# State updates behind the level of 32, level 64 in the first level tensor, gate products one projection later

## The chip, the cores and the metric

One core of a Trainium2 chip runs the whole program; the other seven are idle. The metric is the device time of one execution in microseconds (us). Five engines work side by side: TensorE (PE in the profile; its weight loads are PEld), VectorE (DVE), ScalarE (ACT), GpSimd (POOL) and SyncE (SP, which issues DMAs). Each runs its instructions in the order in which they were put into its queue, and waits where one needs a result of another engine that isn't there.

## The reference, cut to what matters

One layer of a decoder takes 512 prompt tokens and 8 sample tokens (520 columns). The part that the change touches is two recurrences that share one input projection. HGRN2 has 8 heads with 128 keys and values:

```
S_t = diag(f_t) S_{t-1} + k_t outer v_t        o_t = S_t^T q_t
```

For the prompt it is computed in chunks; the 8 samples update a state of 128 x 128 each once. RG-LRU has 8 blocks of 128 channels, each with a causal convolution of width 4 and gates from block-diagonal matrices:

```
xc = causal_conv(xb);  r = sigmoid(blockdiag(xc, wa) + ba);  ig = sigmoid(blockdiag(xc, wx) + bx)
a = exp(-8 r softplus(-lambda));  h_t = a_t h_(t-1) + sqrt(1 - a_t^2) (ig_t xc_t)
o_b = h * gelu(yb)
```

Everything behind it (the merge of both branches, the output projection, the MLP) is left as it is.

## The kernel before, in words

Activations lie with channels on the 128 partitions and the 520 tokens along the free axis. Every projection (`gemm`) yields 128 channels: eight blocks of 128 inputs, for each three products (the weights' high part with the activations' high and low part, and the weights' low part `wlo` with the high part) of two halves of 260 columns, so 48 matmuls of L110. The weights come by DMA to `wst`; ScalarE casts the high part `whi` (L78) and VectorE subtracts it for `wlo` (L81). There are two places, so a projection's weights are split while the one before runs, and its fifth product is the first that reads `wlo`.

The heads come one after the other. Head h projects f, q, the output gate and v. An even head is followed by the projections of two x blocks (`rg_x`): each is evacuated to `xb`, goes through the convolution `xc` on VectorE (L732, and three pairs L735 and L736), is split into `xcs` (ScalarE L158, then VectorE), and enters the block-diagonal products (`blockdiag`, L718): first with `wa`, then with `wx`, three products for each half, whose results ScalarE turns into gates (L132). An odd head has the scans (`rg_scans`) of both blocks between its gate and its v, and the projections of two y blocks (`rg_y`) behind it. The scans use ScalarE functions of several tables, and so there are three table loads in each odd head: for L753 and L754, for the square roots L760, and back for the sigmoids L132.

Within a head (`head_prompt`) the prompt's decays are taken apart by levels of 1, 2, 4, 8, 16, 32 and 64 tokens. Each level multiplies half of the last level tensor by the decays and copies the other half (VectorE L568 and L572) into a new tile `Y` of a ring of four. Small fp32 products of 32 x 32 and 32 x 64 blocks (L582) fill the attention matrix; those of levels 8 to 32 and the state products of the samples form one group. `level(64)` yields the keys that L643 transposes; ScalarE copies these to `kn` (L645), which L649 multiplies by the values. Each head's sample part, `head_sample`, scales a state by f on ScalarE (L527) and adds key times value on VectorE (L528); the values come as `vb`, a broadcast to all partitions through DRAM (v to `vs`, to `vd`, to `vb`).

The program is written in tile form, and a scheduler puts each engine's instructions in order by priority, a simulated timeline and the tiles' dependencies. `urgent` raises the priority, `behind` keeps an instruction behind another in the order without a semaphore, and the small products are chained that way, behind the level and the state update that they read.

Of the kernel before, what the change touches and what calls it, by code (L numbers as in the profile page):

```python
# [6 lines left out]
F32 = mybir.dt.float32  # L7
# [4 lines left out]
OP = mybir.AluOpType  # L12
# [6 lines left out]
T = L + NB  # L19
HALF = T // 2  # L20
KO = D // 128
H = 8
C = 128
# [20 lines left out]
RING = 4  # L44
# [7 lines left out]
class Kernel:  # L52
    def __init__(self, ctx, tc, ins, outs):
# [1 line left out]
        self.i, self.o = ins, outs  # L55
        self.group, self.sigmoids, self.mod_open = None, [], None
        self.ppt_free = True


    def weights(self, specs):  # L60
        self.wspecs = specs
# [51 lines left out]
                    self.behind(self.last_product, after)  # L113

    def gemm(self, keys, acts, extra=0):

        ps = self.pmm.tile([128, 2, 512], F32, name="mm")
        for q, key in enumerate(keys):
            hi, lo = self.take_w(key)
            for k in range(KO):  # L120
                n = q * KO + k
                self.products(ps, (hi[:, k], lo[:, k]), acts[n], n == 0, n == len(keys) * KO - 1, extra)
                if self.mod_open and k == MODK:
                    self.mod_close(self.last_product)
        return ps


    def behind(self, ins, first):
        self.tc.add_manual_dep(ins.ins, first.ins.name, NOSYNC, reason="tables")

    def sigmoid(self, out, x, **kw):
        ins = self.nc.scalar.activation(out, x, AF.Sigmoid, **kw)  # L132
        if self.group:
            self.behind(ins, self.group)
        self.sigmoids.append(ins)
        return ins
# [384 lines left out]
                            vd.rearrange("b v -> (b v)").partition_broadcast(128))  # L521
        return vb

    def head_sample(self, h, st, vb, fkq):
        nc = self.nc
        for b in range(NB):
            nc.scalar.activation(st[:, b], st[:, b], AF.Copy, scale=fkq[:, 0, b:b + 1])  # L527
            last = nc.vector.scalar_tensor_tensor(st[:, b], vb[:, b], fkq[:, 1, b:b + 1], st[:, b], OP.mult, OP.add)  # L528
        nc.sync.dma_start(self.o["hgrn_s"][0, :, h].rearrange("b k v -> k b v"), st)
        return last  # L530

    def head_sample_out(self, h, ev):
        nc = self.nc
# [6 lines left out]
    def head_prompt(self, h, f, X, q, v, og, st, vb, fkq):  # L540
        nc = self.nc
# [14 lines left out]
        def view(t, first_q, first_k, step, n, b):  # L556

            return bass.AP(tensor=t.tensor, offset=t.offset + first_q,
                           ap=[t.ap[0], [T + first_k - first_q, 2], [step, n], [1, b]])

        levels, decay = [X], [f[:, :L], 0]

        def level(b):

            X, (tb, to), n = levels[-1], decay, L // (2 * b)
            Y = self.hg.tile([128, 2, T], F32, name="Y", bufs=RING)
            fac = bass.AP(tensor=tb.tensor, offset=tb.offset, ap=[tb.ap[0], [1, 2], [2, n], [0, b]])
            made = nc.vector.tensor_tensor(view(Y, b, 0, 2 * b, n, b), view(X, b, 0, 2 * b, n, b), fac, OP.mult)  # L568
            if b == 1:
                nc.scalar.copy(view(Y, 0, 1, 2, n, 1), view(X, 0, 1, 2, n, 1))  # L570
            else:
                made = nc.vector.tensor_copy(view(Y, 0, b, 2 * b, n, b), view(X, 0, b, 2 * b, n, b))  # L572
            t2 = tb.rearrange("p (n two) -> p n two", two=2)
            tn = T_[:, to:to + n]
            nc.vector.tensor_tensor(tn, t2[:, :, 0], t2[:, :, 1], OP.mult)
            levels.append(Y)
            decay[:] = tn, to + n
            return made
# [8 lines left out]
        def blocks(after, p, c0, x):  # L587
# [4 lines left out]
            return p[:, c0:c0 + 128].rearrange("p (c t) -> p c t", c=NC)  # L592

        level(1)
        made = [level(2)]
        p = self.pps.tile([128, 512], F32, name="ps")
        for c in range(NC):
# [7 lines left out]
        for b in (1, 2, 4):  # L605
            nc.vector.copy_predicated(a32, self.masks[b], found[b])

        level(4)
        level(8)
        state = self.head_sample(h, st, vb, fkq)  # L610
        level(16)
        made = [level(32), state]
        p = self.pps.tile([128, 512], F32, name="ps")
        p2 = self.ppt.tile([128, 512], F32, name="pt")
        for c in range(NC):
# [4 lines left out]
        for b in range(NB):  # L620
            j, c = 32 * (b % 4), 256 + 128 * (b // 4)
# [10 lines left out]
        nc.scalar.copy(at[:64, :, 64:], p2[:64, :256].rearrange("p (c t) -> p c t", c=NC))  # L632
        ev = self.hg.tile([128, 256], F32, name="sev", bufs=1)
        nc.scalar.copy(ev, p2[:, 256:])
        level(64)
        X, tb = levels[-1], decay[0]
        Q, K = X[:, 0], X[:, 1]
        for j in range(0, 128, 32):
# [71 lines left out]
    def blockdiag(self, w, x, bias):  # L710
        nc = self.nc
        o = self.slot(self.hg, "gate")
        (wh, wl), (xh, xl) = w, x
        for s in range(2):
            c = slice(s * HALF, (s + 1) * HALF)
            ps = self.ppb.tile([128, 512], F32, name="pb")
            for n, (a, b) in enumerate(((wh, xh), (wh, xl), (wl, xh))):
                nc.tensor.matmul(ps[:, :HALF], a, b[:, c], start=n == 0, stop=n == 2)  # L718
            self.sigmoid(o[:, c], ps[:, :HALF], bias=bias)
        return o  # L720

    def rg_x(self, n):

        nc = self.nc
        w = self.blockdiag_w(n)
        ps = self.gemm([(self.i["w_in"][0], 0, 4 * D + n * 128)], self.h)[:, :, :HALF]
        xb = self.slot(self.hg, "xb")
        with self.urgent():
            nc.scalar.copy(self.two(xb), ps)
        xc = self.slot(self.hg, "xc")  # L730
        cw = self.cw
        nc.vector.tensor_scalar(xc, xb, cw[:, 3, n:n + 1], self.cb[:, n:n + 1], OP.mult, OP.add)  # L732
        for j in range(3):
            d = 3 - j
            nc.vector.scalar_tensor_tensor(xc[:, d:L], xb[:, :L - d], cw[:, j, n:n + 1], xc[:, d:L], OP.mult, OP.add)  # L735
            nc.vector.scalar_tensor_tensor(xc[:, L:], self.cbuf[:, :, j, n], cw[:, j, n:n + 1], xc[:, L:],  # L736
                                           OP.mult, OP.add)
        nc.vector.tensor_copy(self.xlast[:, n, 0:3], xb[:, L - 3:L])
        nc.vector.tensor_copy(self.xlast[:, n, 3:11], xb[:, L:])
        xs = self.split(xc, self.hg, "xcs")  # L740
        r = self.blockdiag(w[0], xs, self.ba[:, n:n + 1])
        g = self.blockdiag(w[1], xs, self.bx[:, n:n + 1])
        nc.vector.tensor_tensor(g, g, xc, OP.mult)
        self.rg[n] = r, g

    def rg_scans(self, ns):
# [816 lines left out]
```

## Time and profile before

| | us |
|---|---|
| median of three runs | 1032.24 |
| lowest and highest | 1031.08, 1033.33 |
| the profiled execution | 1032.62 |
| its span, from the first to the last instruction | 1030.6 |
| TensorE busy in the span | 985.0 (96%) |
| VectorE, ScalarE, GpSimd busy | 691.3, 524.2, 112.1 |

In a row of the timeline the first number is the start in us from the span's start, the second the time to the end of the last of the instructions that are grouped in the row; in brackets is the idle time of the engine ahead of it, and what ended it. A row of the waits has the total in us, how often, and the longest. The eight heads with their x and y blocks end at about 440 us.

### The profile page before, as it was taken

To read this page: it belongs to the slowest core of one execution; us is meant where nothing else is said; L and a number is where in the kernel's file an instruction comes from. 1 tells how busy PE (TensorE), PEld (TensorE's weight loads), DVE (VectorE), ACT (ScalarE), POOL (GpSimd) and SP (SyncE) were. 2 spreads that over 40 slices of the span, in tenths; PEclk is the share of its full clock that TensorE was granted. 3 is DMA by queue.
4 is the path that set the end of the run, shared out by engine and by line. 5 is a ranking of instruction groups with operands and counts; after the bars stand their busy time and mean duration, and the time that the engine had idled before them with its cause. 6 is when DMAs were issued, how large, how long until landed. Compare 5 with 4: busy or idle time off the path is not lost.

```text
span 1030.6 us, 23395 instructions
## 1 busy us (share of the span) xinstructions
PE 985.0 (96%) x9620; PEld 956.8 (93%) x9620; DVE 691.3 (67%) x1533; ACT 524.2 (51%) x998; POOL 112.1 (11%) x217
## 2 busy tenths in 40 slices
PE   3899999999899899999999999999999999999995
PEld 1799998999899899998998999999999999999994
DVE  6669697686968687474333347677776776777675
ACT  5545753574466257352222235466556655656653
POOL 3200000000000000020000000011421331232040
PEclk9999999999999999999999999999999999999998
DMA  9944344343434424495755677322672483273242
GB/s 301 283 138 113 119 127 134 90 134 123 113 112 127 117 83 125 122 330 160 230 170 164 216 206 187 88 83 62 134 188 68 94 188 109 53 175 82 63 82 84
DMA packets 214508, 143.65 MB, mean 139 GB/s; under 512 B 6142, under 2 KB 200854, under 8 KB 214394
## 3 DMA queue, kind: packets, MB, share of 16 engines
q1 hardware_dynamic: 204498, 130.24, 42.7%
q0 software_dynamic: 9904, 11.92, 6.1%
q8 instruction: 75, 1.23, 0.5%
q14 instruction: 31, 0.25, 0.1%
HBM read 123.61 MB, written 11.26 MB: 131 GB/s over the span
## 4 chain that ended last, share of the span: by engine, by line
PE 83%; DVE 5%; ACT 3%; DMA 3%; issue 1%; DVEq 0%; ACTq 0%
PE mm L110 60%; PE ps L1101 8%; PE pt L1101 4%; PE pb L1101 2%; PE ps L352 1%; DMA vb<-vd 1%; PE pb L718 1%; DVE wlo L81 1%; PE ps L582 1%; DVE st L528 1%; PE mm L1101 1%; DMA vd<-vs 1%; PE pt L660 1%; PE pt L649 1%; DVE xc L735 1%
## 5 line engine op out<-in xcount | busy, mean ns | idle before, releaser
L110 PE MATMUL mm<-h,whi 128*128 128x260 f32 (+1 forms) x3072 | 508.7, 285 | 1.8 <-ACT X L132 1.2
L110 PEld LDWEIGHTS mm<-h,whi 128*128 128x128 f32 x3072 | 427.2, 189 | 5.0 <-issue 2.5
L110 PE MATMUL mm<-h,wlo 128*128 128x260 f32 (+1 forms) x1536 | 317.3, 285 | 4.5 <-DVE wlo L81 4.5
L78 ACT CAST whi<-wst 128x1024 fp32r<-128x1024 f32 x166 | 173.6, 1049 | 217.3 <-PE mm L110 166.1
L81 DVE TENSOR_TENSOR wlo<-wst,whi 128x1024 fp32r<-128x1024 f32 x166 | 202.9, 1223 | 89.9 <-ACT whi L78 86.8
L110 PEld LDWEIGHTS mm<-h,wlo 128*128 128x128 f32 x1536 | 240.8, 189 | 6.8 <-DVE wlo L81 5.8
L110 PE MATMUL mm<-a,whi 128*128 128x260 f32 x512 | 83.7, 284 | 0.0
L110 PEld LDWEIGHTS mm<-a,whi 128*128 128x128 f32 x512 | 70.5, 189 | 0.9 <-issue 0.8
L110 PE MATMUL mm<-a,wlo 128*128 128x260 f32 x256 | 52.3, 285 | 0.0
L813 POOL DMA_DIRECT2D t<-oaT_d x8 | 4.3, 550 | 389.7 <-ACT whi L78 382.8
L1197 DVE TENSOR_TENSOR f<-f 128x260 f32<-128x260 f32 x64 | 27.3, 427 | 28.9 <-ACT f L1192 28.2
L1189 POOL TENSOR_TENSOR ft<-ft,fsh 128x8 f32<-128x8 f32 x28 | 18.4, 658 | 220.2 <-DVE ft L1183 220.2
L1186 ACT ACTIVATE ft<-ft,fsh 128x512 f32<-128x512 f32 (+2 forms) x36 | 24.0, 676 | 35.9 <-DVE ft L1183 35.9
L110 PE MATMUL mm<-b,whi 128*128 128x260 f32 x256 | 41.6, 284 | 0.0
L568 DVE TENSOR_TENSOR Y<-Y,tb 128x512 f32<-128x512 f32 x48 | 33.1, 690 | 11.5 <-PE ps L582 6.4
L110 PEld LDWEIGHTS mm<-a,wlo 128*128 128x128 f32 x256 | 39.5, 188 | 0.0
L110 PEld LDWEIGHTS mm<-b,whi 128*128 128x128 f32 x256 | 35.0, 188 | 2.5 <-ACT t L132 2.5
L1231 POOL DMA_DIRECT2D ma<-snap x28 | 26.3, 939 | 40.4 <-issue 33.2
L829 DVE TENSOR_TENSOR t<-mm,t 128x520 f32<-128x520 f32 x8 | 5.6, 700 | 37.0 <-PE mm L110 37.0
L1213 POOL DMA_DIRECT2D ma<-snap x28 | 26.1, 931 | 38.6 <-DMA ma<-snap 22.1
L528 DVE SCALAR_TENSOR_TENSOR st<-vb,fkq,st 128x128 f32<-128x128 f32 x64 | 18.1, 348 | 16.6 <-DMA vb<-vd 16.6
L352 PE MATMUL ps<-wm,cT 128*32 128x256 f32 (+1 forms) x256 | 25.5, 523 | 3.6 <-DVE pl L218 2.1
(489 smaller groups left out, 1823.4 us busy)
## 6 DMA issues: line engine op xcount, KB each, us to landing
wst<-in_w_in_dram SPq DMA_DIRECT2D x64, 512.0 KB, 4.6
wm<-in_w_mod_dram SPq DMA_DIRECT2D x8, 2048.0 KB
wst<-in_w_ff_dram SPq DMA_DIRECT2D x64, 256.0 KB, 3.5
wst<-in_w_ff_dram SPq DMA_DIRECT2D x32, 512.0 KB, 4.1
wm<-in_w_mod_dram SPq DMA_DIRECT2D x8, 1024.0 KB
st<-in_state_hgrn_dram SPq DMA_DIRECT2D x8, 512.0 KB
vb<-vd SPq DMA_DIRECT2D x8, 512.0 KB, 4.0
out_dram<-st SPq DMA_DIRECT2D x8, 512.0 KB, 3.4
```

What stands on the lines that cost most here:

```text
L78: ins = self.nc.scalar.copy(hi, st)
L81: self.nc.vector.tensor_tensor(lo, st, hi.bitcast(F32), OP.subtract)
L110: self.last_product = self.nc.tensor.matmul(ps[:, s, :c.stop - c.start], x, y[:, c], start=first and n == 0, stop=last and n == 2)
L352: nc.tensor.matmul(ps[r:r + 32, :n], self.cT[:, k, :], w[:, k, :], start=k < 4, stop=k >= KO - 4)
L528: last = nc.vector.scalar_tensor_tensor(st[:, b], vb[:, b], fkq[:, 1, b:b + 1], st[:, b], OP.mult, OP.add)
L568: made = nc.vector.tensor_tensor(view(Y, b, 0, 2 * b, n, b), view(X, b, 0, 2 * b, n, b), fac, OP.mult)
L1101: ins = self.nc.tensor.matmul(ps, x[:, w], y[:, f], start=j in (1, 7, 2) and k == 0 and n == 0, stop=k == 3 and n == 2, skip_group_check=True)
L1186: nc.scalar.activation(t[:, :p], t[:, :p], AF.Relu, bias=sh[:, 0:1])
L1189: eng.tensor_tensor(t[:, p:], t[:, p:], sh[:, 1:9], OP.add)
L1197: self.nc.vector.tensor_tensor(f[:, n], f[:, a], f[:, b], op)
L1213: nc.gpsimd.dma_start(x[1][:, b], v[:, :n], accum_op=OP.add)
L1231: nc.gpsimd.dma_start(x[t][:, a], s[p], accum_op=OP.add)
```

## The change

Three things. `head_sample` takes the instruction behind which its first VectorE update must stand, now the copy of `level(32)`, and chains the updates. The last level is written into the first level tensor X, whose contents are no longer needed then, and is issued as urgent straight behind the state updates, in the program ahead of the small products of levels 8 to 32. The block-diagonal products of an x block are kept back (`rg_pending`) until the next projection has been issued, and stand behind that projection's last product as written.

```diff
--- before.py
+++ after.py
@@ -55,7 +55,7 @@
         self.i, self.o = ins, outs
         self.group, self.sigmoids, self.mod_open = None, [], None
         self.ppt_free = True
-
+        self.rg_pending = None
 
     def weights(self, specs):
         self.wspecs = specs
@@ -113,6 +113,11 @@
                     self.behind(self.last_product, after)
 
     def gemm(self, keys, acts, extra=0):
+        ps = self.gemm_alone(keys, acts, extra)
+        self.rg_gates()
+        return ps
+
+    def gemm_alone(self, keys, acts, extra):
 
         ps = self.pmm.tile([128, 2, 512], F32, name="mm")
         for q, key in enumerate(keys):
@@ -127,6 +132,7 @@
 
     def behind(self, ins, first):
         self.tc.add_manual_dep(ins.ins, first.ins.name, NOSYNC, reason="tables")
+        return ins
 
     def sigmoid(self, out, x, **kw):
         ins = self.nc.scalar.activation(out, x, AF.Sigmoid, **kw)
@@ -521,13 +527,13 @@
                             vd.rearrange("b v -> (b v)").partition_broadcast(128))
         return vb
 
-    def head_sample(self, h, st, vb, fkq):
+    def head_sample(self, h, st, vb, fkq, after):
         nc = self.nc
         for b in range(NB):
             nc.scalar.activation(st[:, b], st[:, b], AF.Copy, scale=fkq[:, 0, b:b + 1])
-            last = nc.vector.scalar_tensor_tensor(st[:, b], vb[:, b], fkq[:, 1, b:b + 1], st[:, b], OP.mult, OP.add)
+            after = self.behind(nc.vector.scalar_tensor_tensor(st[:, b], vb[:, b], fkq[:, 1, b:b + 1], st[:, b], OP.mult, OP.add), after)
         nc.sync.dma_start(self.o["hgrn_s"][0, :, h].rearrange("b k v -> k b v"), st)
-        return last
+        return after
 
     def head_sample_out(self, h, ev):
         nc = self.nc
@@ -563,7 +569,7 @@
         def level(b):
 
             X, (tb, to), n = levels[-1], decay, L // (2 * b)
-            Y = self.hg.tile([128, 2, T], F32, name="Y", bufs=RING)
+            Y = levels[0] if b == C // 2 else self.hg.tile([128, 2, T], F32, name="Y", bufs=RING)
             fac = bass.AP(tensor=tb.tensor, offset=tb.offset, ap=[tb.ap[0], [1, 2], [2, n], [0, b]])
             made = nc.vector.tensor_tensor(view(Y, b, 0, 2 * b, n, b), view(X, b, 0, 2 * b, n, b), fac, OP.mult)
             if b == 1:
@@ -607,9 +613,10 @@
 
         level(4)
         level(8)
-        state = self.head_sample(h, st, vb, fkq)
         level(16)
-        made = [level(32), state]
+        state = self.head_sample(h, st, vb, fkq, level(32))
+        with self.urgent():
+            made = [self.behind(level(64), state)]
         p = self.pps.tile([128, 512], F32, name="ps")
         p2 = self.ppt.tile([128, 512], F32, name="pt")
         for c in range(NC):
@@ -632,7 +639,6 @@
         nc.scalar.copy(at[:64, :, 64:], p2[:64, :256].rearrange("p (c t) -> p c t", c=NC))
         ev = self.hg.tile([128, 256], F32, name="sev", bufs=1)
         nc.scalar.copy(ev, p2[:, 256:])
-        level(64)
         X, tb = levels[-1], decay[0]
         Q, K = X[:, 0], X[:, 1]
         for j in range(0, 128, 32):
@@ -715,7 +721,7 @@
             c = slice(s * HALF, (s + 1) * HALF)
             ps = self.ppb.tile([128, 512], F32, name="pb")
             for n, (a, b) in enumerate(((wh, xh), (wh, xl), (wl, xh))):
-                nc.tensor.matmul(ps[:, :HALF], a, b[:, c], start=n == 0, stop=n == 2)
+                self.behind(nc.tensor.matmul(ps[:, :HALF], a, b[:, c], start=n == 0, stop=n == 2), self.last_product)
             self.sigmoid(o[:, c], ps[:, :HALF], bias=bias)
         return o
 
@@ -738,9 +744,15 @@
         nc.vector.tensor_copy(self.xlast[:, n, 0:3], xb[:, L - 3:L])
         nc.vector.tensor_copy(self.xlast[:, n, 3:11], xb[:, L:])
         xs = self.split(xc, self.hg, "xcs")
+        self.rg_pending = n, w, xs, xc
+
+    def rg_gates(self):
+        if self.rg_pending is None:
+            return
+        (n, w, xs, xc), self.rg_pending = self.rg_pending, None
         r = self.blockdiag(w[0], xs, self.ba[:, n:n + 1])
         g = self.blockdiag(w[1], xs, self.bx[:, n:n + 1])
-        nc.vector.tensor_tensor(g, g, xc, OP.mult)
+        self.nc.vector.tensor_tensor(g, g, xc, OP.mult)
         self.rg[n] = r, g
 
     def rg_scans(self, ns):
```

Line numbers of the new program are 6 higher up to the levels and 12 higher at the scans (L568 is L574, L760 is L772).

VectorE, head 4, from the level of 16 on. The last figure of a level's shape is its size (16, 32), `a` is the attention's diagonal blocks, `st` the samples' states, `os` their evacuated outputs, `xlast` the convolution's last inputs. Before:

```order
L568 TENSOR_TENSOR Y<-Y,tb 128x2x16x16
L528 SCALAR_TENSOR_TENSOR st<-vb,fkq_660,st 128x128 x5
L604 TENSOR_TENSOR a_3512<-ps,mdiag 128x128
L528 SCALAR_TENSOR_TENSOR st<-vb,fkq_660,st 128x128 x3
L538 COPY os<-pt 128x8
L81 TENSOR_TENSOR wlo<-wst,whi 128x1024
L572 COPY Y<-Y 128x2x16x16
L732 TENSOR_SCALAR xc<-xb,pa 128x520
L738 COPY xlast<-xb 128x3
L739 COPY xlast<-xb 128x8
L606 COPY_PREDICATED a_3512<-mask_237,ps 128x128
L568 TENSOR_TENSOR Y<-Y,tb 128x2x8x32
```

After:

```order
L574 TENSOR_TENSOR Y<-Y,tb 128x2x16x16
L610 TENSOR_TENSOR a_3508<-ps,mdiag 128x128
L578 COPY Y<-Y 128x2x16x16
L544 COPY os<-pt 128x8
L81 TENSOR_TENSOR wlo<-wst,whi 128x1024
L612 COPY_PREDICATED a_3508<-mask_237,ps 128x128
L574 TENSOR_TENSOR Y<-Y,tb 128x2x8x32
L738 TENSOR_SCALAR xc<-xb,pa 128x520
L744 COPY xlast<-xb 128x3
L745 COPY xlast<-xb 128x8
L612 COPY_PREDICATED a_3508<-mask_241,ps 128x128
L578 COPY Y<-Y 128x2x8x32
L534 SCALAR_TENSOR_TENSOR st<-vb,fkq_660,st 128x128 x8
```

The eight updates, which wait for `vb`, stood behind the product of level 16, and now stand behind the copy of level 32, with the split L81 and the start of the convolution ahead of them. What follows after them is L741 and L742 (the convolution's first pair), a mask step, the product of level 64 into X and the next split L81; then the second pair, the copy of level 64 and the third pair. Before, the product of level 64 came behind the small products.

TensorE, head 4, around the small products: `pt` and `ps` are their PSUM tiles, `fkq` the samples' f, k and q, `pb` the block-diagonal results, `mm` a projection. Before:

```order
L110 MATMUL mm<-h,wlo 128x260 x2
L582 MATMUL pt<-Y 32x64 x8
L582 MATMUL pt<-st,fkq_660 32x128 x8
L582 MATMUL ps<-Y 32x32 x40
L718 MATMUL pb<-xcs,bdhlru_wa 128x260
L110 MATMUL mm<-h,whi 128x260 x4
```

After:

```order
L110 MATMUL mm<-h,wlo 128x260 x2
L110 MATMUL mm<-h,whi 128x260
L588 MATMUL pt<-Y 32x64 x8
L588 MATMUL pt<-st,fkq_660 32x128 x8
L588 MATMUL ps<-Y 32x32 x40
L724 MATMUL pb<-xcs,bdhlru_wa 128x260
L110 MATMUL mm<-h,whi 128x260 x3
```

The first block-diagonal product stood right behind the small products and still does. What moved is the number of projection products ahead of the group, seven more now, and the second block's products, which lie further back.

ScalarE, head 5, around its second and third table load; `ag` and `xc` are tiles of the scans, `y` and `e` of y blocks and output gates, `at` and `sev` evacuations of the small products, `g` at its end the keys `kn`. Before:

```order
L760 ACT_TABLE_LOAD
L760 ACTIVATE xc<-xc 128x520 x2
L132 ACT_TABLE_LOAD
L132 ACTIVATE y<-y 128x520
L632 COPY at<-pt 64x4x64
L634 COPY sev<-pt 128x256
L782 ACTIVATE y<-y 128x520
L78 CAST whi<-wst 128x1024
L132 ACTIVATE e<-mm 128x520
L132 ACTIVATE X<-mm 128x520
L132 ACTIVATE y<-y 128x520
```

After:

```order
L78 CAST whi<-wst 128x1024
L768 ACTIVATE xc<-ag 128x520
L639 COPY at<-pt 64x4x64
L641 COPY sev<-pt 128x256
L772 ACT_TABLE_LOAD
L772 ACTIVATE xc<-xc 128x520
L793 COPY y<-mm 128x520
L772 ACTIVATE xc<-xc 128x520
L138 ACT_TABLE_LOAD
L138 ACTIVATE y<-y 128x520
L638 COPY at<-ps 32x4x32 x2
L651 COPY g<-pt 128x512
```

Before, the evacuations of the small products came behind all three loads, and the keys' copy L645 a few rows behind those shown, after `at` again. Now the gates come a projection later, the split's cast L78 stands further up in the row, the evacuations lie ahead of the second load, and the keys' copy (L651) is the seventh row behind it, with the load for the sigmoids between. On TensorE, from the last block-diagonal product of head 5 on, 28 products of projections stand ahead of the small products and 19 between these and the keys' transposes; before, 57 stood between the small products and the transposes.

## The prediction

> **What bounds the kernel.** The page comes first: TensorE is busy for 96% of the span, so only time in which it waits, or runs at a lower clock, can be won.
>
> ```profile
> PE 985.0 (96%) x9620; PEld 956.8 (93%) x9620; DVE 691.3 (67%) x1533; ACT 524.2 (51%) x998; POOL 112.1 (11%) x217
> ```
>
> The view of waits says whom TensorE waited for: total, times, longest. These rows lie in the eight heads:
>
> ```profile
> PE pb L718 <- ACT xcs L158: 5.6, 3, 1.9
> PE mm L110 <- DVE wlo L81: 4.5, 5, 1.3
> ...
> PE pt L643 <- DVE hlast L771: 2.1, 2, 1.3
> ```
>
> L718 is the block-diagonal product, L110 a projection's, L643 the transpose of the last level's keys. Next the clock, from windows of 25 us (fields: length; busy time of PE, PEld, DVE, ACT, POOL; granted clock; DMA share; GB/s). Head 2 lies in the first, head 4 in the second:
>
> ```profile
> 175.00:200.00 25.00, 25.00 (x199) 25.00 (x198) 21.42 (x62) 13.61 (x36) 0.00 (x0) 0.93 0.38 108
> 250.00:275.00 25.00, 21.81 (x362) 21.17 (x361) 17.80 (x49) 8.31 (x15) 0.00 (x0) 1.00 0.47 136
> ```
>
> At 0.93 the stretch lost 0.07 x 25 = 1.75 us; no other in the heads is below 0.99. Then TensorE's timeline in head 4 (the other even heads look alike), with two waits at close quarters:
>
> ```profile
> 259.62 0.64 PE L110 MATMUL mm<-h,whi 128*128 128x260 f32 x4
> 261.59 0.51 PE L110 MATMUL mm<-h,wlo 128*128 128x260 f32 x2 [1.33 <-DVE wlo L81]
> ...
> 264.57 0.40 PE L110 MATMUL mm<-h,wlo 128*128 128x260 f32 x2
> 264.90 0.58 PE L582 MATMUL pt<-Y 128*32 128x64 f32 x14
> ...
> 268.68 0.39 PE L718 MATMUL pb<-xcs,bdhlru_wa 128*128 128x260 f32 x1 [1.86 <-ACT xcs L158]
> ```
>
> A projection's product takes (0.64 - 0.40) / 2 = 0.120 us, as the ends of four and of two differ by two products. Four from 259.62 are over at 260.10, and the next starts at 261.59, 1.49 late: the 1.33 counts from a modelled end, and such a wait costs 0.16 more. So the three rows of waits are worth 5.6, 4.5 + 5 x 0.16 = 5.3 and 2.1 + 2 x 0.16 = 2.4, 13.3 us in all.
>
> **Where these waits come from.** VectorE and ScalarE in head 4:
>
> ```profile
> 253.29 0.69 DVE L568 TENSOR_TENSOR Y<-Y,tb 128x512 f32<-128x512 f32 x1 [1.50 <-PE ps L582]
> 257.94 1.40 DVE L528 SCALAR_TENSOR_TENSOR st<-vb,fkq,st 128x128 f32<-128x128 f32 x5 [3.96 <-DMA vb<-vd]
> ...
> 260.32 1.22 DVE L81 TENSOR_TENSOR wlo<-wst,whi 128x1024 fp32r<-128x1024 f32 x1
> 261.45 0.42 DVE L572 COPY Y<-Y 128x512 f32<-128x512 f32 x1
> 261.79 0.55 DVE L732 TENSOR_SCALAR xc<-xb,pa 128x520 f32<-128x520 f32 x1
> ...
> 262.39 0.30 DVE L606 COPY_PREDICATED a<-mask,ps 128x128 f32<-128x128 uint8 x1
> 262.59 0.69 DVE L568 TENSOR_TENSOR Y<-Y,tb 128x512 f32<-128x512 f32 x1
> 263.19 0.75 DVE L735 SCALAR_TENSOR_TENSOR xc<-xb,pa,xc 128x509 f32<-128x509 f32 x1
> ...
> 263.99 0.30 DVE L606 COPY_PREDICATED a<-mask,ps 128x128 f32<-128x128 uint8 x1
> ...
> 266.65 0.75 DVE L735 SCALAR_TENSOR_TENSOR xc<-xb,pa,xc 128x511 f32<-128x511 f32 x1
> ```
>
> ```profile
> 252.30 1.05 ACT L78 CAST whi<-wst 128x1024 fp32r<-128x1024 f32 x1 [1.53 <-PE mm L110]
> ...
> 267.51 0.59 ACT L729 COPY xb<-mm 128x520 f32<-128x520 f32 x1 [6.89 <-DVE xc L735]
> 268.00 0.63 ACT L158 CAST xcs<-xc 128x520 fp32r<-128x520 f32 x1
> ```
>
> The state updates L528 stand ahead of everything, and VectorE idles 3.96 us for the broadcast `vb`, the longest of its eight waits for it:
>
> ```profile
> DVE st L528 <- DMA vb<-vd: 16.6, 8, 4.0
> ```
>
> The split L81 behind them holds TensorE, and the convolution ends late.
>
> **Even heads.** Start to start, VectorE's steps take: level's product 0.60, its copy 0.34, L81 1.13, L732 with two small copies 0.60, a mask step 0.20, L735 with its small companion 0.80, an update 1.40 / 5 = 0.28. In the new order from 253.29: product 0.60, mask step 0.20, copy 0.34, L538 0.1, L81 1.13. The split is done at 255.7 (its source was ready at 252.30 + 1.05 = 253.35), and TensorE asks for it at 260.1: this wait goes. Mask step, level 32's product, L732's group, mask step and copy take 1.94 more, to 257.6, so the wait for `vb` shrinks from 3.96 to 0.3. From 257.94 follow eight updates 2.2, L735 0.80, mask step 0.20, level 64's product 0.60, L81 1.13, L735 0.80, copy 0.34: the last L735 starts at 264.0, not 266.65. L729 comes 0.86 behind it, L158 another 0.49, and it takes 0.63: `xcs` at 266.0. TensorE was through with the small products at 268.68 - 1.86 = 266.82; without the 1.49, and with seven more projection products ahead of them (0.84), at 266.2. The block-diagonal product still stands right behind the small ones, and has 0.2 us to spare. Gain 5.6, bounds 3.5 (0.7 of each wait stays, as `vb` comes as much later) and 5.6.
>
> **Odd heads.** Level 64 is urgent, so the keys are there when L643 asks: its 2.4 go (0 to 2.4). But L643 and L649, which needs the keys' evacuation (ScalarE, L645), have moved up on TensorE, while on ScalarE the gates come a projection later, and with them the tables that stand ahead of L645. ScalarE and TensorE in head 5:
>
> ```profile
> 301.72 0.47 ACT L132 ACTIVATE gate<-pb,pa 128x260 f32<-128x260 f32 x1
> 302.21 1.28 ACT L753 ACT_TABLE_LOAD   x1
> 303.51 1.35 ACT L753 ACTIVATE ag<-gate,c8n 128x520 f32<-128x520 f32 x2
> 304.76 1.03 ACT L78 CAST whi<-wst 128x1024 fp32r<-128x1024 f32 x1
> 305.70 0.59 ACT L781 COPY y<-mm 128x520 f32<-128x520 f32 x1
> 306.18 0.73 ACT L754 ACTIVATE gate<-gate,c 128x520 f32<-128x520 f32 x1
> 306.81 0.63 ACT L756 ACTIVATE xc<-ag 128x520 f32<-128x520 f32 x1
> 307.34 0.72 ACT L754 ACTIVATE gate<-gate,c 128x520 f32<-128x520 f32 x1
> ...
> 314.88 0.35 ACT L632 COPY at<-pt 64x256 f32<-64x256 f32 x1
> ...
> 320.97 0.53 ACT L631 COPY at<-ps 32x128 f32<-32x128 f32 x2
> 321.52 0.59 ACT L645 COPY g<-pt 128x512 f32<-128x512 f32 x1
> ```
>
> ```profile
> 301.32 0.28 PE L718 MATMUL pb<-xcs,bdllru_wx 128*128 128x260 f32 x1
> ...
> 320.81 0.63 PE L643 MATMUL pt<-ident,Y 128*128 128x128 f32 x4 [1.27 <-DVE hlast L771]
> ...
> 324.39 0.83 PE L649 MATMUL pt<-g 128*128 128x128 f32 x6
> ```
>
> The last gate starts 0.40 behind the last block-diagonal product. From there ScalarE's new order adds: gate 0.49, table load 1.30, L753 1.25, L754, L756, L754 0.63 + 0.53 + 0.62, L78 0.94, L756 0.53, L632 and L634 0.62 (0.35 by the row, less overlap), table load 1.30, L760 0.55, L781 0.48, L760 0.63, table load 1.29, `y` 0.55, L631 0.55, L645 0.59 = 12.85 (L760 and `y` are of L756's size). The keys are there 0.40 + 12.85 = 13.25 behind that product. TensorE, by its new order: 0.12, then 28 projection products 3.36, the small products 264.81 to 266.82 = 2.0, 19 more 2.28, a change of kind 0.08, and L643 to L649 as here 324.39 - 320.81 = 3.58: 11.4. A wait of 1.9, in head 5 and, with the same rows, in head 3: 3.8 lost. Bounds 0 (L645 is ready to run a load and an evaluation earlier than these sums have it, 1.30 + 0.55) and 3 each (L760 waits for VectorE too, by as much as a scan or a split, 1.1).
>
> **Heads 7 and 1.** VectorE's new order in head 7 has both scans ahead of the split that projection 47 needs:
>
> ```profile
> 404.85 1.22 DVE L768 TENSOR_TENSOR_SCAN hs<-ag,gate 128x512 f32<-128x512 f32 x1
> ```
>
> From the end of the second L756, 4.30 behind the gate, come 14.0 us of VectorE's rows: two splits and two scans at 1.13 (4.5), updates 2.2, nine of 0.6 (5.4), copies, mask steps and small ones 1.9. With 0.40, the split is there 18.7 behind the last block-diagonal product; TensorE asks for it 17.4 behind (115 projection products 13.8, small ones 3.5, 0.12): 1.3 lost, bounds 0 and 1.6. In head 1 the like sums leave about 0.45 (0 to 1).
>
> **Smaller parts.** Copy and product of level 64 keep their sizes when they go to X: nothing. Fewer ring tiles only let the next head's levels start earlier, and VectorE (67% busy) hides that. The changes between the two kinds of product grow by four, at 264.90 - 264.81 = 0.09 at most: 0.2, with 0.5 as the bound. No DMA is added; the state's store is issued some 1 to 2 us later, and nobody in the head waits for it.
>
> **The sum.** 13.3 - 3.8 - 1.3 - 0.45 - 0.2 = 7.55. The profiled execution took 1032.62 (span 1030.6 and 2 around it), 0.38 over the median of the runs and within their spread: 1032.62 - 7.55 = 1025.1, with one stretch of low clock in both.
>
> **The clock and tables, page beside row.** The half-clock stretch of head 2 followed a wait of at most 1.9 us, and heads 4 and 6 had such waits without one. The Trainium skill, "TensorE: Matmul & The Clock Gate", the part on the two states, puts the drop behind an idle window of about 3.4 us; the trace disagrees, having one after 1.9. By that page no wait here would cost clock, which is the third rival below. The Trainium skill, "ScalarE: Activation LUTs", "What ACT_TABLE_LOAD costs", counts 1283 ns for the load and 1380 ns of drain. The rows have the load at 1.28, and the next instruction starts 303.51 - 302.21 = 1.30 after it: no drain. By that page the three loads ahead of L645 would make the sum worse by 3 x 1.38 in heads 3 and 5, 8.3 us, which the fourth rival has in its own rows.
>
> **Rivals.** (1) The new waits at L649 and in head 7 do not come, because ScalarE's order leaves it idle less than these sums have it: 1025.1 - 3.8 - 1.3 = 1020.0. For it speaks that ScalarE is 51% busy; against, that the three table loads stand in a row. (2) Nothing is done: the first L718 stays right behind the small products, and `xcs` is late as before: 1025.1 + 5.6 = 1030.7. Against it, 2.65 us less for the last L735. (3) No stretch of low clock in the new run: 1025.1 - 1.75 = 1023.4; the longest waits left are as long as that of head 2, where one in three dropped it. (4) A table load is followed by a stall of its own length when another table comes right behind: 3 x 1.3 more in heads 3 and 5 = 7.8, 1032.9; all rows of loads speak against it. (5) The other side: `vb` lands later than seen. The updates now stand ahead of level 64 and the last convolution step, and only 0.2 is spare: a landing d later costs d - 0.2 in each of heads 2, 4 and 6. From d = 2.7 the gain is gone, from 3.4 the kernel is slower than a measurement's grain (2.3 if each such wait also costs 1.75 of clock). At d = 4: 1025.1 + 3 x 3.8 = 1036.5. Against: the transfer and its place of issue are the same, and head 4, used here, has the longest wait of all eight.
>
> **Chances.** Forecast 0.48; (1) 0.20; (2) 0.11; (3) 0.12; (4) 0.02; (5) 0.07. Forecast, (1) and (3) are faster: 0.80. (2) and (4) lie within 0.2% (2.1 us, about what a measurement can tell): 0.13. (5) slower: 0.07. The likeliest has 1022.5 to 1029 by its bounds; with (1) below and (2) above, 1019.5 to 1030.8.
>
> **What would show it.** Right: no wait of L718 for `xcs` over 0.5 in heads 2, 4, 6; no wait of L643; L649 waiting some 1.9 for ScalarE in heads 3 and 5; the split late by 1.3 in head 7; VectorE's wait for `vb` (16.6 in all) down to a few us. Wrong: `xcs` still late, a wait of several us behind `vb`, or L649 not waiting.

## The result, and the profile after

The changed kernel takes 1023.05 us (median of five runs, 1022.58 to 1025.55) against 1032.24 (1029.36 to 1033.33): a ratio of 0.9919, 95% interval 0.9899 to 0.9939, so 0.8% faster. Its profiled execution took 1022.86, with a span of 1020.9. TensorE's busy time fell by 1.9 us, about what the lowered clock of head 2 had cost; the rest of the 9.7 us of span are waits that went:

```profile
PE 983.1 (96%) x9620; PEld 955.8 (94%) x9620; DVE 688.7 (67%) x1533; ACT 523.3 (51%) x998; POOL 112.0 (11%) x217
```

The waits of TensorE that lie in the heads (total, times, longest), and VectorE's for `vb`, which had been 16.6 us:

```profile
PE pt L655 <- ACT g L651: 3.4, 2, 1.7
...
PE mm L110 <- DVE wlo L81: 1.4, 1, 1.4
```

```profile
DVE st L534 <- DMA vb<-vd: 0.6, 1, 0.6
```

The waits for `xcs` (5.6) and of the keys' transposes (2.1) have no row any more, and the five for the split (4.5) are one. New is L655 (L649 before), as forecast. The window of head 2 that stood at 0.93 is at full clock:

```profile
175.00:200.00 25.00, 25.00 (x213) 24.98 (x212) 18.80 (x55) 14.38 (x40) 0.00 (x0) 1.00 0.28 79
```

The accounts close: 13.3 us of old waits, less 3.4 + 2 x 0.16 and 1.4 + 0.16 of new ones, are 8.0; with the 1.75 of clock 9.75. Between the two profiled executions lie 1032.62 - 1022.86 = 9.76. That they agree to 0.01 is partly luck: from the 97th to the 2593rd projection product, a stretch that takes in the waits of the heads, TensorE's time went from 387.21 to 377.73, so 9.48, and most of the remaining 0.3 lies ahead of it.

In head 4 VectorE no longer stands still ahead of the updates, and the split and the convolution are on time:

```profile
249.72 1.21 DVE L81 TENSOR_TENSOR wlo<-wst,whi 128x1024 fp32r<-128x1024 f32 x1
...
252.46 0.41 DVE L578 COPY Y<-Y 128x512 f32<-128x512 f32 x1
252.79 2.18 DVE L534 SCALAR_TENSOR_TENSOR st<-vb,fkq,st 128x128 f32<-128x128 f32 x8
...
258.76 0.73 DVE L741 SCALAR_TENSOR_TENSOR xc<-xb,pa,xc 128x511 f32<-128x511 f32 x1
```

```profile
259.61 0.59 ACT L735 COPY xb<-mm 128x520 f32<-128x520 f32 x1 [3.77 <-DVE xc L741]
260.10 0.63 ACT L164 CAST xcs<-xc 128x520 fp32r<-128x520 f32 x1
```

```profile
260.18 1.16 PE L588 MATMUL ps<-Y 128*32 128x32 f32 x80
261.27 0.39 PE L724 MATMUL pb<-xcs,bdhlru_wa 128*128 128x260 f32 x1
```

`xcs` is there at 260.10 + 0.63 = 260.73, and the block-diagonal product starts at 261.27, straight behind the small products. In head 5 the keys' copy comes behind all tables, and TensorE waits:

```profile
296.21 0.28 PE L724 MATMUL pb<-xcs,bdllru_wx 128*128 128x260 f32 x1
...
304.09 0.60 PE L649 MATMUL pt<-ident,X 128*128 128x128 f32 x4
309.50 1.16 PE L655 MATMUL pt<-g 128*128 128x128 f32 x8 [1.71 <-ACT g L651]
```

```profile
303.53 1.28 ACT L772 ACT_TABLE_LOAD   x1
304.82 0.64 ACT L772 ACTIVATE xc<-xc 128x520 f32<-128x520 f32 x1
...
306.50 1.28 ACT L138 ACT_TABLE_LOAD   x1
307.79 0.64 ACT L138 ACTIVATE y<-y 128x520 f32<-128x520 f32 x1
308.33 0.51 ACT L638 COPY at<-ps 32x128 f32<-32x128 f32 x2
308.86 0.59 ACT L651 COPY g<-pt 128x512 f32<-128x512 f32 x1
```

The transposes are through at 304.7, and ScalarE is then busy with square roots, a copy, a table load and a sigmoid before it gets to them.

### The profile page after: what moved, and what is told of

Read it like the earlier page. It is cut to its first block, busy times and chain, and to the rows that moved or that the text cites. A ratio compares the mean times of both kernels' runs of the same rounds, so it can differ in the third digit from the quotient of the medians.

```text
span 1020.9 us, 23403 instructions
## 1 busy us (share of the span) xinstructions
PE 983.1 (96%) x9620; PEld 955.8 (94%) x9620; DVE 688.7 (67%) x1533; ACT 523.3 (51%) x998; POOL 112.0 (11%) x217
## 4 chain that ended last, share of the span: by engine, by line
PE 87%; ACT 5%; DVE 3%; issue 1%; DVEq 0%; ACTq 0%
PE mm L110 63%; PE ps L1113 8%; PE pt L1113 4%; PE pb L1113 2%; PE ps L358 1%; PE pb L724 1%; PE ps L588 1%; PE pt L655 1%; PE mm L1113 1%; PE pt L666 1%; PE pt L668 1%; ACT L772 1%; DVE st L534 0%; DVE wlo L81 0%; ACT whi L78 0%
## 5 line engine op out<-in xcount | busy, mean ns | idle before, releaser
L110 PE MATMUL mm<-h,wlo 128*128 128x260 f32 (+1 forms) x1536 | 313.8, 284 | 1.4 <-DVE wlo L81 1.4
L78 ACT CAST whi<-wst 128x1024 fp32r<-128x1024 f32 x166 | 173.7, 1049 | 219.8 <-PE mm L110 165.4
L81 DVE TENSOR_TENSOR wlo<-wst,whi 128x1024 fp32r<-128x1024 f32 x166 | 202.5, 1221 | 95.8 <-ACT whi L78 94.5
L574 DVE TENSOR_TENSOR Y<-Y,tb 128x512 f32<-128x512 f32 x40 | 27.5, 687 | 8.5 <-PE ps L588 7.2
L1204 ACT ACTIVATE f<-ft 128x520 f32<-128x520 f32 (+1 forms) x36 | 20.8, 587 | 14.9 <-POOL ft L1202 12.9
```

The costliest lines, as they stand in the source:

```text
L78: ins = self.nc.scalar.copy(hi, st)
L81: self.nc.vector.tensor_tensor(lo, st, hi.bitcast(F32), OP.subtract)
L110: self.last_product = self.nc.tensor.matmul(ps[:, s, :c.stop - c.start], x, y[:, c], start=first and n == 0, stop=last and n == 2)
L1204: nc.scalar.activation(f, self.two(self.ft)[:, a:a + n], AF.Square)
```

## Experiments

Three questions: which part of the change does the work, what makes the new waits, and what sets off the low clock. Each time is a median of the kernel's runs, and the kernel before ran beside it.

### One part taken away, or alone

The changed kernel with the gate products issued at once:

```diff
 ...
-        self.rg_pending = n, w, xs, xc
+        r = self.blockdiag(w[0], xs, self.ba[:, n:n + 1])
+        g = self.blockdiag(w[1], xs, self.bx[:, n:n + 1])
+        nc.vector.tensor_tensor(g, g, xc, OP.mult)
 ...
```

> The changed kernel without its third part (gate products issued at once, as before). Theory: the third part moves nothing, the scheduler has the five engines' instructions in the same order without it; 1022.9 us as the changed kernel (1022.5 to 1025.5), L655's two waits for ScalarE of 1.7 us still there. Rival: as the prediction had it, the gates that come a projection later push the table loads back and make L655 wait; then without it that wait goes, 1022.9 - 3.7 = 1019.2.

1022.9 us (1022.32 to 1023.66), and the same two waits of L655 (1.50 and 1.69, where the changed kernel has 1.69 and 1.71). The third part moves nothing: without it the scheduler puts every instruction of all five engines in the same order. The rival, which was the prediction's own reason for the late tables, falls. Its counterpart is the kernel before with that part alone:

```diff
+        self.rg_pending = n, w, xs, xc
 ...
-        r = self.blockdiag(w[0], xs, self.ba[:, n:n + 1])
 ...
```

> The kernel before with the third part alone (gate products issued one projection later and kept behind its last product). Theory: the scheduler has them there anyway, so the times are those of the kernel before, 1028.5 to 1035, in steps of 1.7 by how many of the three waits for xcs are followed by a stretch at half clock, and the profile has the same three waits of 1.9 for xcs. Rival: the gates' place matters without the other parts, and the waits for xcs change.

1033.37 (1028.93 to 1035.51), a ratio to the kernel before of 1.0011 (0.9996 to 1.0026): no change. TensorE's three waits for `xcs` are all there.

The kernel before with the first part alone, and with the second alone:

```diff
 ...
-        state = self.head_sample(h, st, vb, fkq)
         level(16)
-        made = [level(32), state]
+        made = [self.head_sample(h, st, vb, fkq, level(32))]
```

> The kernel before with the first part alone (state updates behind the copy of level 32; level 64 stays in a ring tile behind the small products). Theory: this part takes away the late split (5.3) and the late xcs (5.6), and by that the stretch of low clock (1.75); the waits of L643 (2.4) stay: 1032.6 - 12.65 = 1020 to 1022, with no L649 wait, since the transposes stay late. Rival: level 64 is needed as well, the last convolution step still comes behind masks that wait for small products, xcs stays late: 1032.6 - 5.3 = 1027.

```diff
-            Y = self.hg.tile([128, 2, T], F32, name="Y", bufs=RING)
+            Y = levels[0] if b == C // 2 else self.hg.tile([128, 2, T], F32, name="Y", bufs=RING)
 ...
-        made = [level(32), state]
+        level(32)
+        with self.urgent():
+            made = [level(64), state]
 ...
-        level(64)
```

> The kernel before with the second part alone (level 64 into X, urgent, ahead of the small products; state updates where they were, so VectorE still waits 16 us for vb in all). Theory: only the 2.4 of L643 go, and the split and xcs stay late, as level 64 adds 0.9 to the row ahead of them: 1029 to 1034. Rival: the hoisted level carries the gain: 1023 to 1025.

The first alone takes 1025.21 (1023.48 to 1025.43; ratio 0.9924, 0.9897 to 0.9951), the second alone 1019.98 (1019.37 to 1020.75; ratio 0.9879, 0.9857 to 0.9901). Both are misses, the first by 3 us and the second by 9. With the first, L643's waits went too, though level 64 stayed where it was, and the two rows left in the heads are these:

```profile
PE pt L583 <- DVE Y L573: 1.2, 1, 1.2
...
PE mm L110 <- DVE wlo L81: 0.5, 1, 0.5
```

Its profiled execution has 0.69 of the clock in 25 to 30 us and 0.62 in 30 to 35, ahead of the heads; its three runs at 0.993 or 0.994 took 1025.0 to 1025.4, and the one at 0.997, 1023.48. The second part alone was expected to leave the late split and the late `xcs`, and beats the whole change. Its rows:

```profile
PE pt L645 <- DVE X L573: 2.2, 3, 0.7
...
PE mm L110 <- DVE wlo L81: 1.3, 1, 1.3
...
PE pt L645 <- ACT sev L637: 0.7, 1, 0.7
```

```profile
DVE st L529 <- DMA vb<-vd: 4.8, 5, 1.6
```

So the updates still stand at their old place and still wait for `vb`, but 4.8 us in all, and neither the split nor `xcs` in heads 2, 4 and 6 is late: in head 4 the split and the start of the convolution now stand ahead of the product of level 16 and of the updates. Each part makes the scheduler lay out the heads anew, and in either layout VectorE meets `vb` later in its row. On TensorE the two differ: the second part alone has 16 to 71 more projection products ahead of a head's small group than the kernel before, the first alone 8 to 46 fewer. The gains of the parts don't add: by the medians of this comparison (1032.44 before) 7.2 for the first alone, 12.5 for the second alone, and 9.5 for both (no_pending). Part of the 7.2 is the low clock ahead of the heads: from the 97th to the 2593rd projection product the first alone takes 377.70, the changed kernel 377.73, the second alone 375.88. So in the heads the second part, added to the first, gains nothing. The first alone has fewer waits left than the changed kernel and is no faster, so its order costs 3 us elsewhere, where no wait is seen; what they are stays open.

### Is it the wait for vb?

Neither part is needed if that is so. One edge on the kernel before: a head's updates stand behind the next weight split.

```diff
 ...
+            self.updates.append(last)               # in head_sample
 ...
+            for x in self.updates:                  # in take_w, behind the split
+                self.behind(x, self.wlo_ins)
+            self.updates = []
```

> The kernel before with one order edge: each head's state updates stand behind the next weight split (L81) on VectorE; level 64 and the gates as before. Theory: either part of the change works because VectorE no longer stands idle for vb with a split and a convolution behind it, so this edge alone does as much: waits for wlo and xcs under 2 us in all, 1032.4 - 10.9 = 1021 (1019 to 1024). Rival: the particular places of the change are needed (level 32 ahead of the updates or level 64 in X); only the 5.3 of the split go: 1027.

1020.09 (1019.68 to 1022.78), a ratio of 0.9895 (0.9855 to 0.9935). In the heads not one wait of TensorE of 0.1 us or more is left, and VectorE waits for `vb` 1.6 us:

```profile
249.00 0.69 DVE L573 TENSOR_TENSOR Y<-Y,tb 128x512 f32<-128x512 f32 x1 [0.31 <-PE ps L587]
...
250.21 1.22 DVE L82 TENSOR_TENSOR wlo<-wst,whi 128x1024 fp32r<-128x1024 f32 x1
251.35 0.29 DVE L611 COPY_PREDICATED a<-mask,ps 128x128 f32<-128x128 uint8 x1
252.32 2.20 DVE L532 SCALAR_TENSOR_TENSOR st<-vb,fkq,st 128x128 f32<-128x128 f32 x8 [0.68 <-DMA vb<-vd]
```

The split (L82 here) and a few copies fill the time in which `vb` is on its way. One edge gives more than the three parts: three of its four runs, at 0.996 or 0.997 of the clock, took 1019.7 to 1020.3, and no run of the changed kernel was below 1022.1. By the accounts above, no wait at all should come to 1032.62 - 13.3 - 1.75 = 1017.6, and its profiled execution took 1020.26. Its TensorE order has twenty more changes between small and projection products than that of the kernel before (258 against 238), and the trace shows where most of the 2.7 went. In head 1 the samples' state products, which follow each other at 0.02 us in the kernel before, are cut up by projection products: seven times one comes 0.21 to 0.32 behind a projection product, where the next projection product comes 0.12 behind, and six times the way back takes 0.20. That is 0.85 + 1.07 = 1.9 us more than in one row. The other 0.8 wasn't traced.

The other way round, the order left to the scheduler and `vb` made early:

```diff
-                            vd.rearrange("b v -> (b v)").partition_broadcast(128))
+                            self.i["state_hgrn"][0, 0, h, 0:8].rearrange("b v -> (b v)").partition_broadcast(128))
```

> The kernel before with vb loaded from an input that is there from the start, so that the broadcast needn't wait for the values' way through DRAM; leaves out the samples' right values (the transfer is of the same size). Theory: the late vb is the root of the split's and of xcs' lateness; VectorE's wait for vb (16.6) goes, and with it the waits of TensorE for wlo and xcs, 10.9: 1019 to 1023. Rival: the row of work on VectorE is too long by itself; the waits stay: 1028 to 1032.

1022.59 (1022.49 to 1025.46; ratio 0.9924, 0.9897 to 0.9952). There is no wait for `vb`, none for `xcs`, and 0.5 for the split; instead:

```profile
PE pt L582 <- DVE Y L572: 3.1, 3, 1.2
PE pt L643 <- DVE Y L572: 0.7, 3, 0.2
```

The scheduler, which sees the early `vb`, moves the small products up to where VectorE's copy is just late. Both kernels say the same: what held TensorE was a row of VectorE that stood behind a transfer. As each of these edits also reorders other rows, the wait was not taken away with all else equal.

### The new waits

One edge on the changed kernel puts the sigmoid of y, and with it the table load, behind the keys' copy in heads 3 and 5. TensorE's order is the same to the last instruction.

```diff
 ...
-        nc.scalar.copy(kn[:, :L], pk)
+        self.kn = nc.scalar.copy(kn[:, :L], pk)
 ...
-        self.sigmoid(t, t, scale=1.5957691216057308)
+        gelu = self.sigmoid(t, t, scale=1.5957691216057308)
+        if n in (2, 3, 4, 5):
+            self.behind(gelu, self.kn)
```

> The changed kernel with one more order edge: in heads 3 and 5 the sigmoid of y, and so the table load ahead of it, stands behind the keys' copy (L651). TensorE's order is the same. Theory: L655 waits because a table load and a sigmoid (1.85 us) stand ahead of the copy; its two waits go (1.7 + 0.16 each): 1022.9 - 3.7 = 1019.2. Rival: the copy is held by something else (the masks, VectorE), or the later y chain makes a wait elsewhere: 1022 to 1023.

The waits of L655 are gone, as the theory has it, and 1.0 of each 1.85 was gained; the rest came back two steps on:

```profile
308.02 0.59 ACT L651 COPY g<-pt 128x512 f32<-128x512 f32 x1
308.63 1.28 ACT L138 ACT_TABLE_LOAD   x1
```

```profile
PE pt L666 <- DVE g L659: 1.2, 2, 0.6
```

L666 reads the running state that VectorE (L659) forms from L655's result, behind both scans. The median is 1022.77, not the 1019.2 that was expected: three of its four runs have 0.993 of the clock, and the profiled one of them shows a half-clock stretch at 25 to 35 us, ahead of the heads; the one at 0.997 took 1020.66. From the 97th to the 2593rd projection product, which takes in all waits of the heads, it has 375.71 us against 377.73: 2.0 gained.

The wait in head 7 by one more edge, the second scan behind the split that was late:

```diff
 ...
+            if self.wnext_split == 47:
+                self.behind(self.scan, self.wlo_ins)
```

> kn_first with one more edge: in head 7 the second scan stands behind the split that was late there. Theory: the wait for wlo of 1.42 falls by the scan's 1.14, as nothing else in VectorE's row changes: 1020.7 - 1.1 = 1019.5 where the clock stays full after the start. Rival: the later scan makes the y chain late and a wait of like size comes there: 1020.7.

1021.45 (1020.47 to 1023.4). The split's wait fell from kn_first's 1.38 to 0.31, by about one scan (1.13 from start to start), and the transposes of head 7 now wait as long for the copy of level 64:

```profile
395.64 0.51 PE L112 MATMUL mm<-h,wlo 128*128 128x260 f32 x2 [0.31 <-DVE wlo L81]
...
397.87 0.63 PE L651 MATMUL pt<-ident,X 128*128 128x128 f32 x4 [1.12 <-DVE X L580]
```

VectorE's rows lie end to end from 386.4 to 398.3 us there, so one row moved only chooses who waits; the edge also moved some of TensorE's products. From the 97th to the 2593rd product it takes 375.99 us, no less than kn_first's 375.71: nothing is gained. The rival was right on the price, though the new wait is at the copy of level 64 and not in the y chain.

### A version that beats both

From the second part alone, head 7's updates go behind the next split:

```diff
 ...
+            if h == 7:                              # in head_sample; take_w as in b_wlo
+                self.updates.append(last)
```

> The kernel x_only (level 64 into X and urgent, updates where they were) with one more edge: in head 7 the updates stand behind the next split. Theory: the one wait for wlo that x_only has left (1.28 in head 7) goes: 1020.0 - 1.4 = 1018.6. Rival: updates that come later make the small products or the scans late instead: 1020 or more.

1019.67 (1018.17 to 1021.55; ratio 0.9885, 0.9851 to 0.9919). Its two runs at 0.996 of the clock took 1018.2 and 1018.4, where 1018.6 was expected. The split's wait is gone, and what stays in the heads is the transposes' wait for the copy of level 64 (three times, 2.2 us in all). That copy stood behind two steps of the next head's forget gate, so:

```diff
 ...
+        if h in (2, 4, 6):
+            for x in low:                           # the two forget-gate steps
+                self.behind(x, self.level64)        # the copy of level 64
 ...
```

> x_wlo7 with one more edge: in heads 1, 3 and 5 the copy of level 64 stands ahead of the next head's two forget-gate steps (0.94 us) on VectorE; TensorE's order is the same. Theory: the three waits of the keys' transposes for that copy (0.73 each, and 0.16 that the view leaves out) go, and nothing takes their place: 1018.3 - 2.7 = 1015.6 where the clock stays full. Rival: the forget gate or the next head's levels come later and wait instead: 1018.

1018.77 (1016.01 to 1019.46), a ratio to the kernel before of 0.9864 (0.9846 to 0.9882); the changed kernel on the same chip had 0.9909 (0.9891 to 0.9926). One wait of 0.5 us is left in the heads:

```profile
PE pt L546 <- DVE e L690: 0.5, 1, 0.5
```

The run at 0.997 of the clock took 1016.01, where 1015.6 were expected; the other four, at 0.993 or 0.994, 1018.5 to 1019.5. The profiled one of them has its low clock at 25 to 35 us.

### The clock

> The changed kernel once more, beside x_best and the kernel before on one chip. 1022.6 to 1023.1 where the granted clock is full outside the start and end, 1024 to 1026 with one more stretch at half clock. If its waits are shorter than those of the kernel before (1.7 against 1.9) but not its number of them, it should show such a stretch about as often for each wait; rival: only waits of 1.86 set it off, and it shows none in the heads.

1022.6 (1022.1 to 1025.06): five runs at 0.996 of the clock, 1022.1 to 1023.7, and one at 0.992, 1025.06, which has no profile to say where its clock was low. The waits of L655 (1.68 and 1.69) are again without a low clock behind them, in this profile and in the two others of this order. The kernel with the third part alone shows the other side. Its three waits for `xcs` are each 1.86, and the windows of 10 us around them (granted clock third from the end):

```profile
175.00:185.00 10.00, 8.43 (x57) 8.43 (x58) 9.28 (x28) 6.04 (x14) 0.00 (x0) 0.83 0.44 115
265.00:275.00 10.00, 8.14 (x164) 7.89 (x164) 9.33 (x27) 4.70 (x11) 0.00 (x0) 1.00 0.53 143
360.00:370.00 10.00, 8.50 (x58) 8.50 (x59) 9.26 (x29) 6.04 (x15) 0.00 (x0) 0.83 0.22 65
```

The first and the third are followed by a lowered clock, the second isn't; a stretch costs 0.17 x 10 = 1.7 us. Products slow down 1 us behind the first wait:

```profile
176.57 0.39 PE L725 MATMUL pb<-xcs,bdhlru_wa 128*128 128x260 f32 x1 [1.86 <-ACT xcs L165]
176.79 0.63 PE L111 MATMUL mm<-h,whi 128*128 128x260 f32 x4
...
178.34 0.64 PE L111 MATMUL mm<-h,wlo 128*128 128x260 f32 x2
178.78 0.64 PE L111 MATMUL mm<-h,whi 128*128 128x260 f32 x2
```

Two products from 178.34 take 0.44, against 0.24 at full clock. Finer windows show where the clock changes, here around the first and the second wait:

```profile
174.11:177.53 3.42, 1.56 (x61) 1.45 (x53) 2.82 (x8) 1.65 (x4) 0.00 (x0) 1.00 0.38 93
177.53:180.94 3.41, 3.41 (x18) 3.41 (x17) 3.41 (x10) 1.05 (x2) 0.00 (x0) 0.50 0.81 220
...
266.27:269.69 3.42, 1.56 (x103) 1.45 (x95) 2.82 (x8) 1.32 (x4) 0.00 (x0) 1.00 0.17 40
269.69:273.10 3.41, 3.41 (x29) 3.41 (x30) 3.41 (x10) 1.52 (x4) 0.00 (x0) 1.00 1.02 272
```

The low clock lasts one cell of 3.41 us, and all changes of the clock in each of the profiles lie on a grid of such cells: the other stretch in the heads starts at 361.85, 184.32 = 54 x 3.413 behind the first. Where a wait falls on this grid would account for two of the three that were followed by nothing. In four cases of six the wait of 1.86 lies whole in one cell and leaves TensorE busy for 1.55 to 1.56 of it; three of these have a low cell behind them. In heads 4 and 6 of the kernel before a cell's edge divides the wait (1.26 and 0.60, 1.21 and 0.65), TensorE is busy for 2.15 or more in either cell, and nothing follows. The fourth whole one, the second window here, is as idle as the first and was not followed; why stays open.

Together with a stretch ahead of the heads, which some kernels' profiles show, this fits the spread of the kernel before, 1028.5 to 1035.3 over all its runs: its runs at 0.996 of the clock took 1028.5 to 1030.7, those at 0.989 1034.4 to 1035.3. Between runs without such a stretch the change is worth about 7 us (8.0 by the accounts of the two profiles), and the rest is clock.

## Why the prediction was right, point by point

The time came out at 1023.05 for 1025.1, inside the range, and the waits went and came as forecast; the clock did not. What held, and what didn't:

**Even heads.** Right. The wait for `vb` in head 4 shrank to nothing (0.3 forecast), the split was done at 249.72 + 1.21 = 250.9, the last step of the convolution started 10.3 behind the product of level 16 (10.7 in the sum), and `xcs` had 0.5 to spare, where the sum gave 0.2. So the 5.6 and 5.3 are gained in full.

**Odd heads.** The number held: the keys were there 309.45 - 296.21 = 13.24 us behind the last block-diagonal product (13.25 forecast), and TensorE asked 309.50 - 1.87 - 296.21 = 11.42 behind it (11.4). The waits were 1.7 each, and 0.16. The steps between agree as well: the sum has the second table load start 0.40 + 6.91 = 7.31 behind that product, at 303.52, and it starts at 303.53. The reason given for it fell: "the gates come a projection later" is not the doing of the third part, which moves nothing; the other two parts move the transposes up on TensorE and the tables by the scheduler's layout. An order that is compared before and after says what moved, not which edit moved it; the kernel without that edit does.

**Heads 7 and 1.** The split in head 7 was there 397.57 + 1.22 - 379.78 = 19.0 behind the last block-diagonal product (18.7), and TensorE asked for it 17.5 behind (17.4): 1.42 lost, 1.3 forecast. In head 1 no wait of 0.1 us or more is seen; the 0.45 was wrong.

```profile
379.78 0.29 PE L724 MATMUL pb<-xcs,bdllru_wx 128*128 128x260 f32 x1
...
398.85 0.51 PE L110 MATMUL mm<-h,wlo 128*128 128x260 f32 x2 [1.42 <-DVE wlo L81]
```

```profile
397.57 1.22 DVE L81 TENSOR_TENSOR wlo<-wst,whi 128x1024 fp32r<-128x1024 f32 x1
```

**The sum.** The term that was mis-sized is the clock: the forecast had one low stretch in both kernels, while 13 of the 15 runs of the new order (the changed kernel twice, and the one without its third part) are at 0.996 or 0.997 of the clock, 1022.1 to 1023.7. That is the third rival, 1025.1 - 1.75 = 1023.4. With 0.45 for head 1 the 2.2 us of difference are accounted for. The forecast took the new waits of 1.9 for as dangerous as those of 1.86; they came out at 1.5 to 1.7, and in three profiles of this order, six such waits, none was followed by a lowered clock, while three of the six waits of 1.86 in the profiles of the kernel before and of the one with the third part were. Four of the six lie whole in a cell of the clock's grid and leave TensorE busy for 1.71 to 1.73 of its 3.41 us, against 1.55 to 1.56 with a wait of 1.86. Whether the line lies between these, or four are too few to tell, stays open.

**The other rivals.** The new waits did come, so the first fell; the second (nothing is done) fell with the rows for `xcs`, though for the third part it is true. A stall behind table loads isn't there: 303.53 to 304.82 is 1.29 for a load to the next instruction. The Trainium skill, "ScalarE: Activation LUTs", "What ACT_TABLE_LOAD costs", adds a drain of 1380 ns to each load, and these rows disagree. `vb` was not late (0.6 us in one head), so the slower side did not come up. That a ring with one tile less to serve costs nothing wasn't tried by itself.

**What the prediction did not ask** is whether the parts add. It took the change as one layout and was right on it, but credited updates and level 64 with separate gains. In the heads the first alone does as much as the whole change, and the second alone more.

## What to carry to other kernels

When an engine in order stands idle for a transfer and a shared chore (here a weight split) is queued behind it, one order edge that puts the chore first can be worth as much as a rewrite: b_wlo's single edge gave 1020.1 where the three parts gave 1023.0. Where a scheduler lays out the program, take each part away by itself: one part of three moved no instruction, and the other two, each meant for its own wait, removed each other's. After a wait is gone, follow the chain two steps on, since half or all of it came back there (L666, head 7).

## What the runs showed of the hardware

A lowered TensorE clock followed three of six idle times of 1.86 us in the heads, for 3.41 us at half speed (1.7 us lost each), and only where the idle time lay whole in one cell of a grid of 3.41 us on which the clock changes. The Trainium skill, "TensorE: Matmul & The Clock Gate", "Why this matters for your kernels", asks for no idle gaps over some 3 us; here 1.86 was enough, at times, and the rule as it stands would have passed these gaps. Five of the profiles also show 6.83 us at half clock from 26.5 to 27.8 us on, behind several idle times of TensorE of 0.3 to 1.1 us each; the others don't. By the granted clock of the runs, runs of one kernel are 2 to 3 us apart for this (1016.0 and 1018.5 to 1019.5 for the fastest one), which is as much as a whole wait that one tries to remove. A small group of transposes leaves the first projection products behind it slower by 0.08 us: in kn_first four of them take 0.72 there and 0.64 elsewhere.

```profile
217.60 0.72 PE L110 MATMUL mm<-h,whi 128*128 128x260 f32 x4
...
218.40 0.64 PE L110 MATMUL mm<-h,whi 128*128 128x260 f32 x4
```
